# Modulation vectors of a two-layer backbone: other column groups, and another engine for the second layer

## The chip, the cores and the metric

The kernel runs on one core of one Trainium2 chip. The metric is the device time of one execution in microseconds (us); the figure for the kernel before is the median of three runs.

## The reference

Two layers work on 512 latent tokens and 256 context tokens of width 1024, all in float32. Each layer first forms modulation vectors, one set for the latent stream's conditioning vector `c` and one for the context's `c_ctx`:

```python
def ada_mod(cond, w_mod, b_mod):
    return jnp.split(jax.nn.silu(cond) @ w_mod + b_mod, N_MOD, axis=-1)   # w_mod: 1024 x 6144
...
    sh_a, sc_a, gt_a, sh_m, sc_m, gt_m = ada_mod(cond, w_mod, b_mod)
    # pre-norm, input product, three head groups (gated delta rule | global attention | windowed attention)
    x = x + gt_a * (jnp.concatenate([o_a, o_b, o_c], axis=-1) @ w_out)
    x = x + gt_m * sq_relu_mlp(modulate(x, g_mlp, sh_m, sc_m), w_mlp_in, w_mlp_out)
```

The context stream goes the same way in the first layer; in the second it only serves as keys, values and states. The modulation vectors depend on `c`, `c_ctx` and the weights alone.

## The kernel before

Activations are held with features on partitions. Large products are made of float32 parts rounded for the tensor engine: every weight tile of 128x1024 is split into a high and a low part (`weight`, `split`: a copy on ScalarE, a subtraction on VectorE), and `mm3` issues three matmuls for one product. `fm_steps` makes one slice of 128 output features with 24 matmuls of 512 columns (latent) and 24 of 256 (context).

Nothing is issued where it is written. The program is recorded as a list of operations (`Program.add`) with an estimated duration each (`cost`); `layout` then gives every operation a rank, the length of what has to follow it, and plays the five engines forward in time: the operation with the highest rank that is ready and finds memory goes next. The order that results is what each engine gets, as a fixed list. Memory is by kind of tile (`KINDS`: width, and numbers of slots that are always there or in two regions X and Y that change hands between mixers and MLP). `sm`, the staging tile of the modulation weights, has two slots in region X, in the phases of the input products and the mixers only.

One layer is: input products beside the first part of the delta rule; a tail with the rest of the delta rule (`pre`, `scan_step`, `finish`, unit by unit, each state needing the one before) and the attention; the output projection; the MLP, in four rounds of eight slices of hidden features (`w1`) and eight output slices (`w2`). The profile has layer 0's MLP from 810 to 1350 us and layer 1's from 1990 us to the end.

`mod_steps` forms a third (16 columns of 128 features) of a layer's modulation vectors: 16 weight tiles `w_mod` of 128x1024, and for each, two matmuls with the conditioning vectors as the 32-column stationary operand and 512 weight columns streaming. Outputs of 32 rows go to partitions 32j of one PSUM tile, so each matmul uses one of four column groups of the array:

```python
for k in range(KT):
    for hf in range(2):
        st = self.stage(self.a["w_mod"][L.l, r, k, hf], ...)
        for q in range(2):
            j = hf * 2 + q
            nc.tensor.matmul(ps[32 * j:32 * j + 32, :], self.cs[:, k, :], st[:, q * 512:q * 512 + 512], ...)
```

A copy, four transposes and additions of the bias follow, and `aa`, the factors of the norms. The first third of layer 0 is made at the very start. `run` records the others behind the attention: layer 0's second and third third and layer 1's first in layer 0, layer 1's second and third in layer 1. All instructions carry line 674, the helper that issues; tiles tell them apart: `sm` modulation weights, `cs` conditioning vectors, `b` and `h` split activations and hidden features, `w` split weights, `lb` and `kaq` parts of the delta rule's `pre`.

Of the kernel before, what the change touches and what calls it, by code (L numbers as in the profile page):

```python
# [19 lines left out]
P = 128  # L20
# [5 lines left out]
# units of the delta rule: the token tiles that the two directions take at the same time (context first)  # L26
# [7 lines left out]
# Memory by kind of tile: elements per partition, whether rounded for the tensor engine, slots that are always there, and  # L34
# those in two regions that change with the phase (input products, mixers, MLP): X (mixers and before | MLP) and Y
# (input products and MLP | mixers).
# [8 lines left out]
    "pre": (0, False, 0, 1, 0, 0, 0), "inv": (0, False, 0, 1, 0, 0, 0),  # L45
# [3 lines left out]
# how long (ns) before its time, as the length of what follows tells it, an instruction may take memory  # L49
AHEAD = (1e9, 1e9, 1e9, 1e9, 1e5)  # L50
# kinds of which there is little for that
HOARD = ("g", "sm", "t", "u", "a", "r", "kaq", "kv")
# which copies of transposed weights VectorE does, ScalarE the others
# [12 lines left out]
def _constants():  # L66
# [35 lines left out]
    # from here on they are loaded where they are needed  # L102
# [20 lines left out]
# order of the streamed weight tiles of a layer: each [128, 1024] float32  # L123
# [3 lines left out]
def lay_out(inp):  # L127
    """numpy layout only: every array that the chip reads, in its float32 type."""
# [48 lines left out]
class Layer:  # L177
    """What belongs to one layer: small state, arrays in DRAM."""
# [8 lines left out]
class View:  # L187
    """A part of a tile: what the scheduler has to know of it, and how to get it from the real tile."""
# [83 lines left out]
class Tile:  # L272
    """A tile that gets its memory when the program is laid out in time."""
# [18 lines left out]
class Op:  # L292
    __slots__ = "phase", "n", "eng", "name", "args", "kw", "preds", "succs", "tiles", "dur", "moved", "fn", "wait", "ready", "rank", "start", "end", "table", "dense"
# [12 lines left out]
class Program:  # L306
    """Instructions in the order of the arithmetic; laid out in time by the length of what follows each, within the
    memory that there is, and then issued in that order."""

    def __init__(self):  # L310
        self.ops, self.tiles, self.phase, self.latest = [], [], 0, {}
        self.tokens, self.name, self.count = [], "", {}
# [9 lines left out]
    def job(self, name):  # L322
        """A job of this name: each takes its memory after the one of that name before it."""
# [4 lines left out]
    @contextmanager  # L328
    def token(self, kind):
        """At most so many of these at a time as the kind has slots."""  # L330
# [14 lines left out]
    def add(self, eng, name, args, kw):  # L345
# [28 lines left out]
        op.table = None  # L374
# [5 lines left out]
    def cost(op, out, ins):  # L380
        """Estimated time (ns) that it holds its engine; for a transfer, also that of the queues."""
        psum = any(v.tile.kind in ("ps", "pu") for v in ins)
        n = out.cols
        if op.eng == PE:
# [3 lines left out]
            if ins[0].dt == F32R:  # L388
                return k / 2.4 + 2.5, 0
# [19 lines left out]
    def epochs(self):  # L409
        """How often each region has changed at every phase."""  # L410
# [8 lines left out]
    def layout(self):  # L419
# [6 lines left out]
        # a job that needs a token goes on when one of those before it ends  # L426
# [4 lines left out]
        for k, l in chains.items():  # L431
            n = KINDS[k][2] + KINDS[k][3] + max(KINDS[k][5:])
            for t, q in zip(l, l[n:]):
                if t.ops[-1] < q.ops[0]:
                    later.setdefault(t.ops[-1], []).append(q.ops[0])
        for o in reversed(ops):
            own = o.dur + (o.moved + 1550 if o.eng == SP else 0)
            o.rank = own + max((LATE[o.eng][ops[s].eng] + ops[s].rank for s in o.succs + later.get(o.n, [])), default=0.0)
        slotted = [t for t in self.tiles if t.kind in KINDS]
        self.epochs()  # L440
        # slots by kind and place: always there (0), region X (1), region Y (2)
# [8 lines left out]
        # tiles of a time of a region that have to be there, or are  # L450
# [12 lines left out]
        def enter(r, e, now):  # L463
            """Region r changes to its time e, if what it held is done with."""
# [20 lines left out]
        def places(t, now):  # L485
            """(free since, place, slot) that the tile may have."""
# [20 lines left out]
                    # what has been free for the shortest time; a region that changes before what is always there  # L507
# [11 lines left out]
        # what would take memory long before its time  # L519
# [4 lines left out]
        while len(order) < len(ops):  # L524
# [31 lines left out]
            # it goes  # L556
# [1223 lines left out]
```

## Time and profile before

| | |
|---|---|
| median of three runs | 2350.1 us (2349.28 to 2351.54) |
| span of the profiled execution | 2364.2 us |
| time around the span | not shown; the profiled execution's own time is taken as its span |
| TensorE busy | 2185.3 us (92%) |
| VectorE busy | 1419.7 us (60%) |
| ScalarE busy | 907.5 us (38%) |
| GpSimd busy | 592.8 us (25%) |

Busy times are sums over stages with different limits, so the table by stage is the one to read. A matmul of a float32 operand that is not rounded leaves two records, one for each pass. A matmul's recorded duration includes its way through the array, and records overlap.

### The profile page before, as it was taken

What the parts mean: (1) busy time and instruction counts of PE and PEld (TensorE: products, weight loads), DVE (VectorE), ACT (ScalarE), POOL (GpSimd) and SP (SyncE); (2) the same over time, 40 slices, a digit from 0 to 9 for tenths busy, and PEclk for the clock granted to TensorE, in tenths of its full rate; (3) what the DMA queues carried; (4) which work ended last, traced back from release to release, by engine and by line L of the source; (5) the groups of instructions that cost most, each with busy time, mean ns of one, the idle gap of its engine ahead of it and who ended that gap; (6) DMA issues with size and microseconds to landing.
All of it is one profiled execution on the core that took longest, in us unless ns stands there. A gap on an engine that the chain in (4) does not pass through costs nothing. (4 is left out here: it accounts for less than half of the span.)

```text
span 2364.2 us, 46388 instructions
## 1 busy us (share of the span) xinstructions
PE 2185.3 (92%) x18408; PEld 1685.5 (71%) x18408; DVE 1419.7 (60%) x3471; ACT 907.5 (38%) x1748; POOL 592.8 (25%) x1170
## 2 busy tenths in 40 slices
PE   6997999699998899999999899999679988999999
PEld 2785788455646788888888777687536556777777
DVE  4788878867764542332323488999966755334333
ACT  4754423345542431222222375544324444222221
POOL 0274455635320000000000016657653300000000
PEclk7998999789998999999999999999779999999999
DMA  7343324675353121212212325343563332322322
GB/s 274 95 137 89 96 79 127 177 215 179 123 177 101 45 70 58 76 46 71 72 45 76 103 58 166 96 133 101 149 186 120 126 107 72 106 89 94 102 90 80
DMA packets 170744, 260.58 MB, mean 110 GB/s; under 512 B 44448, under 2 KB 107424, under 8 KB 170528
## 3 DMA queue, kind: packets, MB, share of 16 engines
q1 hardware_dynamic: 170528, 257.64, 34.9%
q8 instruction: 144, 2.36, 0.4%
q14 instruction: 72, 0.59, 0.1%
HBM read 220.26 MB, written 37.32 MB: 109 GB/s over the span
## 5 line engine op out<-in xcount | busy, mean ns | idle before, releaser
L674 PE MATMUL ps<-b,w 128*128 128x512 f32 (+1 forms) x3936 | 846.6, 363 | 19.1 <-ACT b L674 10.8
L674 PEld LDWEIGHTS ps<-b,w 128*128 128x128 f32 x3936 | 658.6, 192 | 149.3 <-ACT b L674 13.0
L674 PE MATMUL ps<-h,w 128*128 128x512 f32 (+1 forms) x2304 | 480.7, 357 | 1.9 <-DVE w L674 0.9
L674 PEld LDWEIGHTS ps<-h,w 128*128 128x128 f32 x2304 | 381.5, 188 | 75.0 <-DVE w L674 4.9
L674 ACT ACTIVATE w<-st 128x1024 fp32r<-128x1024 f32 x192 | 198.3, 1055 | 594.4 <-PE ps L674 589.5
L674 DVE TENSOR_TENSOR w<-st,w 128x1024 fp32r<-128x1024 f32 x192 | 236.2, 1258 | 237.3 <-PE ps L674 175.0
L674 POOL TENSOR_TENSOR lb<-l,cst 128x72 fp32r<-128x72 f32 (+7 forms) x768 | 244.9, 355 | 90.7 <-ACT l L674 59.6
L674 ACT ACTIVATE g<-ps 128x512 f32<-128x512 f32 (+3 forms) x286 | 149.8, 540 | 240.1 <-PE ps L674 232.6
L674 DVE SCALAR_TENSOR_TENSOR x<-ps,mod,x 128x512 f32<-128x512 f32 (+1 forms) x120 | 77.0, 658 | 272.2 <-PE ps L674 272.1
L674 PE MATMUL ps<-w,b 128*128 128x256 f32 x1536 | 229.9, 296 | 2.5 <-DVE w L674 2.4
L674 PEld LDWEIGHTS ps<-w,b 128*128 128x128 f32 x1536 | 201.1, 194 | 13.6 <-DVE w L674 4.0
L674 POOL TENSOR_TENSOR g<-g 128x16 f32<-128x16 f32 x12 | 2.3, 226 | 721.9 <-ACT g L674 721.9
L674 DVE TENSOR_TENSOR q<-q,u 128x16 f32<-128x16 f32 (+4 forms) x360 | 133.1, 370 | 22.9 <-ACT u L674 17.7
L674 PE MATMUL ps<-sm,cs 128*32 128x512 f32 x344 | 122.7, 685 | 23.9 <-DMA sm<-w_mod 18.1
L674 DVE TENSOR_TENSOR g<-g 128x512 f32<-128x512 f32 (+3 forms) x112 | 57.8, 541 | 123.1 <-ACT h L674 119.8
L674 DVE SCALAR_TENSOR_TENSOR g<-ps,par,g 128x510 f32<-128x510 f32 (+3 forms) x176 | 106.0, 617 | 7.2 <-ACT g L674 6.4
L674 PE MATMUL ps<-cst,g 128*128 128x128 f32 (+1 forms) x502 | 88.5, 286 | 10.3 <-DVE g L674 6.1
L674 ACT ACTIVATE u<-pu 64x256 f32<-64x256 f32 (+2 forms) x128 | 55.6, 437 | 106.3 <-PE pu L674 93.4
L674 ACT ACTIVATE g<-ps,t 128x256 f32<-128x256 f32 (+2 forms) x144 | 75.3, 532 | 51.0 <-DVE t L674 44.0
L674 POOL TENSOR_TENSOR v<-u,gt 64x256 f32<-64x256 f32 x80 | 52.1, 651 | 142.3 <-DVE t L674 58.2
L674 DVE TENSOR_REDUCE t<-ps 128x2 f32<-128x512 f32 (+3 forms) x104 | 63.2, 622 | 38.6 <-PE ps L674 38.1
L674 PEld LDWEIGHTS ps<-cst,g 128*128 128x128 f32 (+1 forms) x502 | 56.5, 141 | 41.1 <-ACT g L674 15.2
(139 smaller groups left out, 2724.3 us busy)
## 6 DMA issues: line engine op xcount, KB each, us to landing
st<-w SPq DMA_DIRECT2D x128, 512.0 KB, 4.1
sm<-w_mod SPq DMA_DIRECT2D x86, 512.0 KB, 4.3
st<-w_qkv SPq DMA_DIRECT2D x24, 512.0 KB, 4.8
st<-w_tm SPq DMA_DIRECT2D x24, 512.0 KB, 3.8
kv<-kv SPq DMA_DIRECT2D x96, 128.0 KB, 3.5
u<-gd SPq DMA_DIRECT2D x88, 128.0 KB, 3.6
kaq<-kq SPq DMA_DIRECT2D x80, 128.0 KB, 3.2
st<-w_out SPq DMA_DIRECT2D x16, 512.0 KB, 4.5
```

Of the source, the lines that this page charges most:

```text
L674: getattr(engines[o.eng], o.name)(*[real(x) for x in o.args], **{k: real(x) for k, x in o.kw.items()})
```

## The change

Three edits.

1. In `mod_steps`, a weight tile now feeds four matmuls of 256 columns, one in each of the four column groups, instead of two of 512 in two groups; the two halves of a third land side by side in the PSUM tile. This is now used for layer 0 only.
2. Layer 1's modulation vectors are formed in layer 0's MLP by `mod_pieces`: 12 pieces of 512 outputs, each made on VectorE by multiplying eight weight tiles of 128x512 with a per-partition scalar and adding up, for both conditioning vectors (16 operations), then summed over partitions on TensorE with a matrix of ones, copied, transposed and added to the bias. `mlp` takes one piece with every second slice of hidden features until the 12 are used, that is in three of its four rounds. The pieces have a memory kind of their own, `mp` (four slots in the MLP), and the rank of the TensorE work beside which they are recorded (`paced`).
3. The planner's estimate for a rounded matmul of k columns becomes k/2.25 + 4 ns instead of k/2.4 + 2.5.

```diff
+    "mp": (512, False, 0, 0, 4, 0, 0),
...
-                return k / 2.4 + 2.5, 0
+                return k / 2.25 + 4.0, 0
...
+            if o.paced:
+                o.rank = max(o.rank, beside)
+            elif o.eng == PE:
+                beside = o.rank
...
-            for k in range(KT):
-                for hf in range(2):
+            for hf in range(2):
+                for k in range(KT):
...
-                    for q in range(2):
-                        j = hf * 2 + q
-                        nc.tensor.matmul(ps[32 * j:32 * j + 32, :], self.cs[:, k, :], st[:, q * 512:q * 512 + 512],
-                                         start=k == 0, stop=k == KT - 1)
+                    for j in range(4):
+                        nc.tensor.matmul(ps[32 * j:32 * j + 32, 256 * hf:256 * hf + 256], self.cs[:, k, :],
+                                         st[:, j * 256:j * 256 + 256], start=k == 0, stop=k == KT - 1)
...
+    def mod_pieces(self, L):
+        nc = self.nc
+        o, _ = _PAR["b_mod"]
+        for r in range(3):
+            for x in range(4):
+                with self.p.job("mod piece"), self.p.paced():
+                    acc = [self.tile("mp"), self.tile("mp")]
+                    for k in range(KT):
+                        st = self.tile("mp")
+                        self.load(st, self.a["w_mod"][L.l, r, k, x // 2][:, x % 2 * 512:x % 2 * 512 + 512])
+                        for cond in range(2):
+                            c = self.cs[:, k, cond:cond + 1]
+                            if k == 0:
+                                nc.vector.tensor_scalar(acc[cond], st, c, None, op0=ALU.mult)
+                            else:
+                                nc.vector.scalar_tensor_tensor(acc[cond], st, c, acc[cond], op0=ALU.mult, op1=ALU.add)
+                    ps = self.pu()
+                    for cond in range(2):
+                        nc.tensor.matmul(ps[32 * cond:32 * cond + 32, :], self.C("ones")[:, 0:32], acc[cond],
+                                         start=True, stop=True)
+                    sb = self.tile("mp")
+                    self.act(sb[:64], ps[:64], AF.Copy)
+                    tp = self.pu((P, 4, 64))
+                    for b in range(4):
+                        nc.tensor.transpose(tp[:, b], sb[:64, b * P:(b + 1) * P], self.C("ident")[:64, :64])
+                    at = r * 16 + 4 * x
+                    for cond in range(2):
+                        self.tt(L.mod[:, cond, at:at + 4], tp[:, :, 32 * cond], L.pt[:, o + at:o + at + 4], ALU.add)
+                if x == 3:
+                    self.mod_scales(L, r)
+                yield
...
+                if s % 2:
+                    next(beside, None)
...
-            self.mod_steps(L, (1, 2))
             if not L.last:
-                self.mod_begin(layers[L.l + 1])
-                self.mod_steps(layers[L.l + 1], (0,))
+                self.mod_steps(L, (1, 2))
...
-                acc = self.mlp(L, who, xs, y, W)
+                self.mod_begin(layers[L.l + 1])
+                acc = self.mlp(L, who, xs, y, W, beside=self.mod_pieces(layers[L.l + 1]))
```

`mod_scales` holds the lines that formed `aa` in `mod_steps`, unchanged.

## Rows read from the trace of the kernel before

**Rows 1.** page, part 1: engine, busy us (share), number of instructions

```profile
PE 2185.3 (92%) x18408; PEld 1685.5 (71%) x18408; DVE 1419.7 (60%) x3471; ACT 907.5 (38%) x1748; POOL 592.8 (25%) x1170
```

**Rows 2.** busy time by stage: stretch, length, busy us by engine, PEclk, DMA

```profile
430.00:725.00 295.00, 260.69 (x3206) 153.54 (x3202) 215.18 (x785) 126.92 (x358) 123.53 (x273) 0.91 0.56 167
...
810.00:1350.00 540.00, 539.00 (x3060) 468.41 (x3058) 192.94 (x287) 134.45 (x216) 0.00 (x0) 1.00 0.20 66
1350.00:1690.00 340.00, 309.25 (x3691) 249.25 (x3689) 297.38 (x763) 181.74 (x317) 192.01 (x376) 0.96 0.39 114
1690.00:1935.00 245.00, 208.17 (x2564) 126.74 (x2564) 171.13 (x589) 99.14 (x278) 92.52 (x193) 0.88 0.44 132
```

**Rows 3.** the same view, instructions of the tile sm alone

```profile
430.00:725.00 295.00, 68.84 (x192) 8.97 (x192) 0.91 0.56 167
1690.00:1790.00 100.00, 18.95 (x48) 2.12 (x48) 0.74 0.56 158
1690.00:1935.00 245.00, 44.08 (x128) 5.48 (x128) 0.88 0.44 132
```

**Rows 4.** chain of waits from 1690 to 1935 us, shares by line

```profile
by line: PE ps L674 39.8%; PE pu L674 18.3%; DMA sm<-w_mod 10.3%; DVE t L674 6.0%; DVE q L674 3.6%; DMA u<-gd 3.1%; DVE g L674 2.8%; DMA r<-kC 2.8%; DMA a<-kB 2.2%; issue 2.1%; DVE u L674 2.0%; DVE s L674 1.1%; POOL u L674 0.9%; DVE kaq L67
```

**Rows 5.** waits from 430 to 725 us: us, times, longest

```profile
PEld ps L674 <- DMA sm<-w_mod: 9.1, 6, 2.6
...
PE ps L674 <- DMA sm<-w_mod: 5.1, 5, 1.7
```

**Rows 6.** timeline of TensorE in layer 0's mixers: start, length, what

```profile
472.00 1.05 PE L674 MATMUL ps<-sm,cs 128*32 128x512 f32 x2 [1.68 <-DMA sm<-w_mod]
...
474.04 1.04 PE L674 MATMUL ps<-sm,cs 128*32 128x512 f32 x2
...
705.52 1.05 PE L674 MATMUL ps<-sm,cs 128*32 128x512 f32 x4
```

**Rows 7.** timeline of TensorE in the prologue

```profile
39.88 1.05 PE L674 MATMUL ps<-sm,cs 128*32 128x512 f32 x4
```

**Rows 8.** timeline of GpSimd: starts of the bursts on lb

```profile
1456.58 4.20 POOL L674 TENSOR_TENSOR lb<-l,cst 128x72 fp32r<-128x72 f32 x16
...
1489.77 8.24 POOL L674 TENSOR_TENSOR lb<-l,cst 128x72 fp32r<-128x72 f32 x24 [4.02 <-ACT l L674]
...
1798.23 7.56 POOL L674 TENSOR_TENSOR lb<-l,cst 128x72 fp32r<-128x72 f32 x28 [2.02 <-ACT l L674]
...
1856.75 6.51 POOL L674 TENSOR_TENSOR lb<-l,cst 128x72 fp32r<-128x72 f32 x24 [11.48 <-ACT l L674]
```

**Rows 9.** groups of VectorE, 800 to 1345 us: busy, mean ns | idle

```profile
L674 DVE TENSOR_TENSOR w<-st,w 128x1024 fp32r<-128x1024 f32 x63 | 75.1, 1222 | 96.4 <-PE ps L674 68.2 <-issue 20.4 <-ACT w L674 7.7
...
L674 DVE TENSOR_TENSOR h<-g,h 128x512 fp32r<-128x512 f32 x32 | 21.5, 687 | 0.4
...
L674 DVE TENSOR_TENSOR h<-g,h 128x256 fp32r<-128x256 f32 x32 | 13.1, 421 | 0.6
...
L674 DVE SCALAR_TENSOR_TENSOR g<-x,amul,g 128x512 f32<-128x512 f32 x8 | 5.7, 744 | 2.7 <-ACT g L674 2.7
```

**Rows 10.** timeline of TensorE around six transposes of 64 rows

```profile
61.64 0.59 PE L674 MATMUL ps<-cst,g 64*128 64x64 f32 x6
62.15 0.50 PE L674 MATMUL ps<-b,w 128*128 128x512 f32 x1
```

**Rows 11.** waits of TensorE's weight loads, 810 to 1350 us

```profile
PEld ps L674 <- DVE w L674: 2.4, 4, 0.9
```

**Rows 12.** DMA issues, 810 to 1350 us: KB each, median us to landing

```profile
st<-w SPq DMA_DIRECT2D x58, 512.0 KB, 3.9
...
x<-x SPq DMA_DIRECT2D x8, 256.0 KB, 2.4
```

**Rows 13.** busy time in the second MLP

```profile
2050.00:2100.00 50.00, 50.00 (x215) 39.67 (x214) 16.65 (x18) 8.87 (x10) 0.00 (x0) 1.00 0.28 95
```

**Rows 14.** busy time in the first part of layer 1's tail

```profile
1690.00:1790.00 100.00, 75.69 (x883) 44.24 (x884) 71.46 (x207) 28.45 (x70) 51.17 (x98) 0.74 0.56 158
```

More of the change, by code (lines that the diff above doesn't have):

```diff
@@ L292 @@
 class Op:
-    __slots__ = "phase", "n", "eng", "name", "args", "kw", "preds", "succs", "tiles", "dur", "moved", "fn", "wait", "ready", "rank", "start", "end", "table", "dense"
+    __slots__ = "phase", "n", "eng", "name", "args", "kw", "preds", "succs", "tiles", "dur", "moved", "fn", "wait", "ready", "rank", "start", "end", "table", "dense", "paced"
 PE, ACT, DVE, POOL, SP = range(5)
@@ L311, in __init__ @@
         self.ops, self.tiles, self.phase, self.latest = [], [], 0, {}
-        self.tokens, self.name, self.count = [], "", {}
+        self.tokens, self.name, self.count, self.pace = [], "", {}, False
         for e, n in enumerate(("tensor", "scalar", "vector", "gpsimd", "sync")):
@@ L326, in job, with paced @@
         self.name, self.count = old
+    @contextmanager
+    def paced(self):
+        self.pace = True
+        yield
+        self.pace = False
     @contextmanager
@@ L373, in add @@
         op.dense = ins[0].shape[0] / P * (1.0 if outs[0].cols > 64 else 0.6) if eng == PE else 0
-        op.table = None
+        op.table, op.paced = None, self.pace
         if eng == ACT:
@@ L435, in layout @@
                     later.setdefault(t.ops[-1], []).append(q.ops[0])
+        beside = 0.0
         for o in reversed(ops):
@@ L818, in mod_steps @@
         nc = self.nc
-        mod, pm, aa = L.mod, L.pt, L.aa
+        mod, pm = L.mod, L.pt
         o, _ = _PAR["b_mod"]
@@ L835, in mod_steps @@
                 nc.tensor.transpose(tp[:, b * P:(b + 1) * P], sb[:, b * P:(b + 1) * P], self.C("ident"))
-            v = tp.rearrange("p (b j s) -> p b j s", b=4, j=4)
-            bm = pm[:, o + r * 16:o + r * 16 + 16].rearrange("p (j b) -> p b j", j=4)
+            v = tp.rearrange("p (f b j s) -> p f j b s", f=2, b=2, j=4)
+            bm = pm[:, o + r * 16:o + r * 16 + 16].rearrange("p (f j b) -> p f j b", f=2, j=4)
             for cond in range(2):
-                ov = mod[:, cond, r * 16:r * 16 + 16].rearrange("p (j b) -> p b j", j=4)
-                self.tt(ov, v[:, :, :, cond], bm, ALU.add)
@@ L841, in mod_steps @@
-            for w, (sc, gn) in enumerate(((8, "g_attn"), (32, "g_mlp"))):
-                if sc // 16 == r:
-                    go, _ = _PAR[gn]
-                    for cond in range(2):
-                        nc.vector.scalar_tensor_tensor(aa[:, w, cond, :], mod[:, cond, sc:sc + 8], 1.0,
-                                                       pm[:, go:go + 8], op0=ALU.add, op1=ALU.mult)
+                ov = mod[:, cond, r * 16:r * 16 + 16].rearrange("p (f j b) -> p f j b", f=2, j=4)
+                for f in range(2):
+                    self.tt(ov[:, f], v[:, f, :, :, cond], bm[:, f], ALU.add)
@@ new lines, in mod_steps, with mod_scales @@
+            self.mod_scales(L, r)
+    def mod_scales(self, L, r):
+        for w, (sc, gn) in enumerate(((8, "g_attn"), (32, "g_mlp"))):
+            if sc // 16 == r:
+                go, _ = _PAR[gn]
+                for cond in range(2):
+                    self.nc.vector.scalar_tensor_tensor(L.aa[:, w, cond, :], L.mod[:, cond, sc:sc + 8], 1.0,
+                                                        L.pt[:, go:go + 8], op0=ALU.add, op1=ALU.mult)
+    def mod_pieces(self, L):
[15 more added lines that the diff above has]
+                    ps = self.pu()
+                    for cond in range(2):
+                        nc.tensor.matmul(ps[32 * cond:32 * cond + 32, :], self.C("ones")[:, 0:32], acc[cond],
[9 more added lines that the diff above has]
+                if x == 3:
+                    self.mod_scales(L, r)
+                yield
@@ L941, in mlp @@
     @job("mlp")
-    def mlp(self, L, who, xs, y, W, after=None):
+    def mlp(self, L, who, xs, y, W, after=None, beside=iter(())):
         acc = dict.fromkeys(who)
```

## The prediction

> **What bounds the kernel now.** First the page's busy table: TensorE is busy 92% of 2364.2 us, VectorE 60%, the rest less [rows 1]. That average mixes stages, so the next view is the table of busy time by stage [rows 2]. In the first MLP (810 to 1350 us) TensorE is busy 539 of 540 us and VectorE 193: whatever is added to TensorE there lengthens it one for one, while VectorE has room. In the tails of the two mixer stages (430 to 725 us in layer 0, 1690 to 1935 us in layer 1) TensorE is busy 260.7 of 295 and 208.2 of 245 us (88 and 85%), with VectorE at 215.2 and 171.1 (73 and 70%): loaded, but broken up by dependencies. The same table kept to the tile `sm` shows that the modulation matmuls lie in just these two stretches: 68.8 and 44.1 us of TensorE's time [rows 3], 48 tiles in the first and 32 in the second, so 1.43 and 1.38 us a tile.
>
> Are those matmuls on the path there, or do they only fill holes? The chain of waits says that in layer 1 they are on it: of 245 us, 10.3% (25 us) is the wait for a `w_mod` transfer itself, and 58% is TensorE's own work, the modulation matmuls among it [rows 4]. The chain as recovered doesn't reach back to layer 0, so there I read the waits: TensorE's two queues stood 9.1 and 5.1 us for `sm<-w_mod` [rows 5], and the stage is 88% full. TensorE runs its list in order, so each such wait holds up the delta rule's and attention's matmuls listed behind it.
>
> **The change, part by part.** All terms are in the profiled execution's own time. Its span is 2364.2 us; nothing around it is shown, and the runs' median of 2350.1 is 0.994 of it.
>
> *Four column groups in layer 0.* In TensorE's timeline a 512-column product issued alone takes 1.05 and 1.04 us for its two recorded passes (472.00 and 474.04 us), and both products of a weight tile, in two column groups, issued together, also take 1.05 us, all four records (705.52 us) [rows 6]. So groups do run side by side, and half the columns in twice the groups should be half of that, some 0.55 us a tile when the four stand together. The 1.43 us measured per tile contains split pairs and low clock; I halve it to 0.72. Bounds: 0.55 (never split) and 1.43 (always split, nothing gained).
>
> *Prologue.* The first third is bound by its transfers; only what follows the last one counts. The last tile takes 1.05 us from 39.88 us on [rows 7] and becomes about 0.5 shorter; the three before it may gain 0.3 each; two more additions of 16 columns on VectorE cost less than the 0.5 us gained. I take -0.5 us, between nothing and -1.5.
>
> *Tail of layer 0's mixers.* 16 of 48 tiles leave (layer 1's first third) and 32 cost 0.72 instead of 1.43: TensorE sheds 68.8 - 23 = 46 us and would need 215, as much as VectorE's 215 [rows 2, 3]. How much of that shortens the stage? Today's busiest engine reaches 88%; with two engines equally loaded and the same chains I expect less, 80%: 215/0.80 = 269, -26 us. Bounds: 215/0.88 = 244 (-51), and, if chains alone set the length, half of the 14.2 us of waits (-7).
>
> *Tail of layer 1's mixers.* All 32 tiles leave: 208.2 - 44.1 = 164 us on TensorE; VectorE's 171 becomes the larger [rows 2, 3]. 171/0.80 = 214, -31 us. Bounds: 171/0.85 = 201 (-44); at the other end the recurrences of the delta rule alone. Their period shows in GpSimd's bursts on `lb`, one a unit: 33 us apart while input products run beside them (1456.58 to 1489.77), but 58 us for the last interval of this tail (1798.23 to 1856.75) [rows 8]. So the recurrence has been stretched and can shrink; I keep -12 (half of the chain's 25 us of transfer waits) as the small end. No view tells how the planner will reorder what is left.
>
> *The first MLP receives the second layer's 48 tiles* as 12 pieces. On VectorE: 192 operations of 128x512. The nearest row, scalar_tensor_tensor with both tensors in SBUF, takes 744 ns [rows 9]; the 24 plain multiplies are not shown, and I charge them the same (below: nothing, 18 us less). 192 x 0.744 = 143 us; with the present 193 that is 336 of some 565, 60%: hidden behind TensorE as an average. But they come in the halves of the MLP where the hidden slices are formed: this stretch has 64 weight slices, 540/64 = 8.4 us each, so two take TensorE 16.8 us [rows 2] and VectorE 6.9 (twice 1222 + 2 x 687 + 2 x 421 ns [rows 9]), and a piece asks 11.9: 18.8 in 16.8. The excess must wait for the following half, which has more room: 193 - 32 x 3.44 = 83 us used there of 270.
>
> On TensorE, in a stage with no hole: two 32-column products over 512 columns, side by side, 1.05 us as in [rows 6]; four transposes, 0.4 of the 0.59 us that six of that size took [rows 10]; and the break in the stream. *Weighed against a rule:* in that row the 128-row stream goes on at 62.15 us, 0.51 us after the transposes began, so the switch of shape costs under 0.15 us beyond them [rows 10]. The Trainium skill, page "TensorEngine Tiling (Array Packing)", section "Key Properties", says that changing the tiling mode drains the engine and gives no price; two switches a piece would by that rule be on top of the sum; by the row they are under 24 x 0.15 = 3.6 us, and are in it. So 12 x (1.05 + 0.40 + 0.15) = 19 us. Each piece's first product also waits for VectorE's last sum and its transposes for ScalarE's copy; before, TensorE's weight loads waited only 2.4 us for VectorE in this whole stage [rows 11]. I add 0.5 us a piece, 6 us: +25 us together. Bounds: +15 (partly side by side) and +67 (4 us of wait a piece, about the landing time of a 512 KB transfer, 3.9 us [rows 12]).
>
> *Queues.* 48 loads of 512 KB become 96 of 256 KB on SyncE, one list with the MLP's weights. A load waits there for one of two staging slots, and weight loads stand behind it; these run up to two slices (17 us) ahead, against 2.4 us for a 256 KB landing in this stage [rows 12]. Nothing charged; if that cover were gone, the 48-matmul stream would wait, which is the upper bound above. ScalarE's 12 copies are hidden (134 of 540 us busy [rows 2]).
>
> *The planner's new price* of a rounded matmul, 512/2.25 + 4 = 231.6 ns, is what the trace has: 215 of these matmuls in 50 us, 233 ns each [rows 13], against 215.8 in the old formula. It moves instructions everywhere, above all in the stages with TensorE at 91% (50 to 430, 1350 to 1690 us). No row prices that: from nothing to the idle that one such stage has (340 - 309 = 31 us [rows 2]) either way; as each list order has waits of its own, I take 0, within 15 either way.
>
> **Sum:** -0.5 - 26 - 31 + 25 + 0 = -32.5: 2331.7 us in the profile, times 0.994 is 2317.7. I forecast 2318 us, 1.4% less.
>
> **Rivals.**
> *The removed matmuls were filling.* If the tails are bound by recurrence and softmax chains, only waits come back: -0.5 - 8 - 25 + 25 = -8.5, 2342 us. For it: 37 us of TensorE idle in the layer 1 tail in spite of the filler. Against: the chain in [rows 4]. 14%.
> *The clock falls.* Without filler TensorE has longer pauses in the first 100 us of layer 1's tail, where it was granted 0.74 of full clock already, that is 1.2 GHz for half the time [rows 14]. If all of that ran at 1.2 GHz, its other work there (75.7 us busy less 19 of modulation [rows 3, 14]) would lengthen by the half that now runs at 2.4, some 25 us: -32.5 + 25, 2343 us. The Trainium skill's "TensorE: Matmul & The Clock Gate", section "Why this matters for your kernels", says that pauses between bursts return the engine to the lower clock. By that rule this rival would hold; the rows agree in kind, yet attention, which is independent of the recurrence, can move into the pauses. 6%.
> *Slower: VectorE's sums arrive late in the MLP.* TensorE stands 4 us at every piece's product: +67 instead of +25, sum +9.5, 2360 us. It decides from about 3.2 us a piece. For it: 18.8 us asked in 16.8. Against: the sums have 60% of VectorE, and a late piece need only be late in the list. 12%.
> *Better:* both tails at today's 88 and 85%, -51 and -44, with +25: 2280 us; halfway there, 2299 or less, 12%.
> *The spread does nothing* (four groups serialized): layer 0's gain falls by half, 2331 us; inside my range, in the forecast's chance, as is a reordering within 15 us.
>
> **How the numbers follow.** The forecast, 2300 to 2336, has 54%; better 12; filling 14; clock 6; slower 12; the remaining 2 a reordering that costs more. About 0.2% (4.7 us) is what a measurement of this kernel tells from no change. Faster by more than that: 54 + 12 + most of 14 + 6, 0.82; slower 0.13; between, 0.05. The range leaves out the slower rival and the far end of the better one: 2288 to 2350.
>
> **What would show it.** Right: no `sm` tile after 725 us and the out projection of layer 1 some 30 us sooner after its MLP; tiles of eight records in about 0.55 us in layer 0; the first MLP 20 to 30 us longer with TensorE still over 97% busy and VectorE near 60%. Wrong: TensorE waiting for `mp` sums for microseconds at each piece; the tail of layer 1 still near 245 us with new idle time in place of `sm`; granted clock below 0.7 there.

## The result: 1.5% slower, where 1.4% faster was forecast

The changed kernel takes 2387.2 us (median of four runs, 2377.7 to 2390.1) against 2349.7 us for the kernel before in the same comparison: a ratio of 1.0148, interval 1.0117 to 1.0180. The forecast of 2318 and its range up to 2350 were both wrong. The profiled execution after has a span of 2387.9 us against 2364.2, 23.7 longer; the median of before lies 14 us under its own profiled span, which is also longer than every timed execution of that kernel on record (2338.1 to 2359.3 us). So some 14 us of any difference to these stages of before may be that one execution, and the averages over several kernels further down weigh more.

The page of the changed kernel: busy time by engine, then the costliest group that is new, then the DMA issues that are new. L687 is the helper that was L674.

```profile
PE 2159.1 (90%) x18492; PEld 1695.3 (71%) x18492; DVE 1539.6 (64%) x3687; ACT 904.6 (38%) x1749; POOL 604.1 (25%) x1170
...
L687 DVE SCALAR_TENSOR_TENSOR mp<-mp,cs,mp 128x512 f32<-128x512 f32 x168 | 118.4, 746 | 47.6 <-DMA mp<-w_mod 47.5
...
mp<-w_mod SPq DMA_DIRECT2D x96, 256.0 KB, 2.7
```

Against [rows 1], TensorE is 26 us less busy and the kernel is longer all the same; VectorE has 120 us more. The table of busy time by stage, changed kernel, answers to [rows 2]: layer 0's tail, its MLP, layer 1's input products, its tail.

```profile
440.00:708.00 268.00, 224.77 (x2983) 150.73 (x2984) 196.68 (x707) 120.37 (x345) 101.48 (x230) 0.85 0.49 148
...
812.00:1380.00 568.00, 562.49 (x3103) 467.30 (x3102) 289.38 (x458) 138.77 (x220) 0.00 (x0) 1.00 0.31 99
1380.00:1745.00 365.00, 322.90 (x3967) 260.60 (x3967) 320.66 (x816) 181.73 (x323) 220.79 (x416) 0.94 0.38 109
1745.00:1957.00 212.00, 167.36 (x2148) 121.54 (x2148) 144.68 (x530) 93.05 (x264) 72.22 (x154) 0.77 0.25 74
```

The same table for the tile `sm` alone answers to [rows 3]: layer 0's tail, the stretch after it, layer 1's tail.

```profile
440.00:708.00 268.00, 33.30 (x256) 8.31 (x256) 0.85 0.49 148
708.00:1388.00 680.00, 0.00 (x0) 0.00 (x0) 0.98 0.32 103
1745.00:1957.00 212.00, 0.00 (x0) 0.00 (x0) 0.77 0.25 74
```

The reader sees what the forecast asked for: no `sm` after layer 0, tails of 268 and 212 us where there were 295 and 245, an MLP filled to 99% by TensorE with VectorE at 51%. What it did not ask for is in the line of 365 us: the input products of layer 1, whose instructions no edit touches, were 340. To avoid stretches chosen by eye, the table below cuts every run at events of TensorE's timeline: mixers from the first input product of a layer to the first product of its output projection, MLP from there to the first input product of layer 1. Input products end with the last `ps<-w,b`, and the last row ends with the last matmul.

| us | before | after | difference |
|---|---|---|---|
| layer 0 mixers: input products + tail | 375 + 307 | 391 + 271 | +16 - 36 |
| output projection and first MLP | 633 | 680 | +47 |
| layer 1 mixers: input products + tail | 321 + 255 | 353 + 218 | +32 - 37 |
| layer 1 projection and MLP | 424 | 424 | 0 |

The four differences of the mixers sum to -25, the MLP gives +47: +22 of the 23.7. So two things failed: the tails' gain was mostly given back in the stages ahead of them, and the pieces cost nearly twice their forecast. By the medians the kernels are 37.5 us apart; with +47 in the MLP that leaves some 10 us of gain for the mixers, and the 25 hold for these two executions only.

**The pieces on TensorE.** Its timeline in the first MLP of the changed kernel, round one piece (idle time ahead of a group, and who ended it, in brackets):

```profile
845.12 1.04 PE L687 MATMUL pu<-mp,cst 128*32 128x512 f32 x2 [0.86 <-DVE mp L687]
846.10 0.61 PE L687 MATMUL ps<-b,w 128*128 128x512 f32 x2
846.64 1.04 PE L687 MATMUL pu<-mp,cst 128*32 128x512 f32 x2
847.62 1.43 PE L687 MATMUL ps<-b,w 128*128 128x512 f32 x6
848.98 0.46 PE L687 MATMUL pu<-cst,mp 64*128 64x64 f32 x4
```

The two 32-column products do not stand together: ordinary matmuls lie between, and each takes its 0.98 us alone (845.12 to 846.10). So it is in ten of the twelve pieces; two show the four records in one group of 1.05 us. From the starts of all matmuls between 840 and 1360 us I work out the price of a piece, as time from one start to the next: the 40 product records of ten pieces hold 17.6 us and the 40 transposes 4.6, 2.2 us a piece; and the 2750 ordinary matmuls there are 1.6 to 6.8 ns longer each on average than the same kinds in before (233.8, 234.0, 118.6 and 118.8 ns, 840 to 1340 us), 10 us in all, 1.0 a piece. That makes 3.2 us a piece, 39 for twelve.

Those 10 us stand mostly at the changes of shape. Where a 32-column product begins inside the ordinary stream (18 places), the ordinary matmul ahead of it takes a median 91 ns more to the next start than its kind in before, and the first one behind it 104 ns more; round the transposes it is 92 and 103. (The product's own second record takes 523 ns where records inside a group take 453.) These places sum to 6.4 of the 10 us. Waits ahead of the products are 1.9 us, and 1.9 us are spread over ordinary matmuls that border no piece. `after_old_price`, `after_ranks` and `after_one_tile`, described below, have the same medians to 2 ns.

The remaining 8 are mostly waits at the norms ahead of the MLP and behind it, as the waits of TensorE from 708 to 1385 us show (us, times, longest):

```profile
PE ps L687 <- DVE g L687: 6.7, 2, 4.7
PE ps L687 <- DVE b L687: 5.6, 3, 2.4
PE ps L687 <- ACT b L687: 4.2, 2, 3.2
PE pu L687 <- DVE mp L687: 1.5, 2, 0.9
```

The same stage of before, 726 to 1358 us:

```profile
PE ps L674 <- ACT b L674: 5.3, 2, 4.4
PE ps L674 <- DVE g L674: 4.4, 2, 2.6
```

That is 16.5 us for `g` and `b` against 9.7, 7 more: 5 at the norm ahead of the MLP and 2 at the next layer's, behind it. For the late sums of `mp` TensorE waited 1.5 us in all: VectorE wasn't late at the pieces.

**The spread.** TensorE in layer 0's tail, changed kernel:

```profile
463.20 1.08 PE L687 MATMUL ps<-sm,cs 128*32 128x256 f32 x8
...
643.05 0.63 PE L687 MATMUL ps<-sm,cs 128*32 128x256 f32 x6
643.61 0.49 PE L687 MATMUL ps<-r,asel 16*128 16x512 f32 x1
644.03 0.63 PE L687 MATMUL ps<-sm,cs 128*32 128x256 f32 x4
644.59 0.44 PE L687 MATMUL pu<-lb,bdb 128*128 128x384 f32 x1
644.96 0.62 PE L687 MATMUL ps<-sm,cs 128*32 128x256 f32 x2
...
662.37 0.64 PE L687 MATMUL ps<-sm,cs 128*32 128x256 f32 x8
```

Six records (three groups) start and end in the same 0.6 us as two, and a whole tile of eight takes 0.64 at 662 us, where the granted clock is 1.00, so groups do run side by side, near the 0.55 us forecast. But many tiles are split into parts of six, four and two records with other matmuls between, and others run at a lower clock (1.08 us for eight at 463 us, where 0.54 was granted). 32 tiles take 33.3 us of TensorE, 1.04 each, not 0.72.

### The profile page after: what moved, and what is told of

It reads as the page before. It is cut to its first block, busy times and chain, and to the rows that moved or that the text cites. A ratio compares the mean times of both kernels' runs of the same rounds, so it can differ in the third digit from the quotient of the medians.

```text
span 2387.9 us, 46928 instructions
## 1 busy us (share of the span) xinstructions
PE 2159.1 (90%) x18492; PEld 1695.3 (71%) x18492; DVE 1539.6 (64%) x3687; ACT 904.6 (38%) x1749; POOL 604.1 (25%) x1170
## 5 line engine op out<-in xcount | busy, mean ns | idle before, releaser
L687 PE MATMUL ps<-b,w 128*128 128x512 f32 (+1 forms) x3936 | 846.2, 363 | 33.0 <-ACT b L687 12.3
L687 PEld LDWEIGHTS ps<-b,w 128*128 128x128 f32 x3936 | 650.7, 191 | 181.1 <-issue 30.3
L687 PE MATMUL ps<-h,w 128*128 128x512 f32 (+1 forms) x2304 | 480.0, 358 | 1.2 <-ACT w L687 0.9
L687 PEld LDWEIGHTS ps<-h,w 128*128 128x128 f32 x2304 | 379.8, 188 | 78.5 <-ACT w L687 6.3
L687 ACT ACTIVATE w<-st 128x1024 fp32r<-128x1024 f32 x192 | 198.8, 1056 | 611.1 <-PE ps L687 595.9
L687 DVE TENSOR_TENSOR w<-st,w 128x1024 fp32r<-128x1024 f32 x192 | 235.6, 1249 | 207.2 <-PE ps L687 133.8
L687 POOL TENSOR_TENSOR lb<-l,cst 128x72 fp32r<-128x72 f32 (+7 forms) x768 | 249.3, 360 | 68.6 <-ACT l L687 51.9
L687 PE MATMUL ps<-w,b 128*128 128x256 f32 x1536 | 240.4, 300 | 5.6 <-DVE w L687 3.1
L687 DVE SCALAR_TENSOR_TENSOR x<-ps,mod,x 128x512 f32<-128x512 f32 (+1 forms) x120 | 77.3, 658 | 247.5 <-PE ps L687 247.5
L687 PEld LDWEIGHTS ps<-w,b 128*128 128x128 f32 x1536 | 208.9, 199 | 16.4 <-issue 5.1
L687 ACT ACTIVATE g<-ps 128x512 f32<-128x512 f32 (+3 forms) x283 | 147.8, 538 | 166.2 <-PE ps L687 153.1
L687 POOL TENSOR_TENSOR g<-g 128x16 f32<-128x16 f32 x12 | 2.3, 225 | 770.0 <-ACT g L687 770.0
L687 DVE TENSOR_TENSOR q<-q,u 128x16 f32<-128x16 f32 (+4 forms) x360 | 147.5, 410 | 14.1 <-ACT u L687 7.5
L687 DVE SCALAR_TENSOR_TENSOR mp<-mp,cs,mp 128x512 f32<-128x512 f32 x168 | 118.4, 746 | 47.6 <-DMA mp<-w_mod 47.5
L687 DVE SCALAR_TENSOR_TENSOR g<-ps,par,g 128x510 f32<-128x510 f32 (+3 forms) x176 | 105.6, 617 | 4.2 <-ACT g L687 3.6
L687 PE MATMUL ps<-cst,g 128*128 128x128 f32 (+1 forms) x490 | 93.5, 304 | 13.9 <-ACT g L687 11.6
L687 ACT ACTIVATE u<-pu 64x256 f32<-64x256 f32 (+2 forms) x128 | 55.3, 437 | 118.8 <-PE pu L687 100.5
L687 ACT ACTIVATE g<-ps,t 128x256 f32<-128x256 f32 (+2 forms) x144 | 75.5, 531 | 63.2 <-DVE t L687 52.8
L687 ACT ACTIVATE g<-g 128x512 f32<-128x512 f32 (+2 forms) x123 | 65.7, 550 | 62.3 <-DVE g L687 46.8
L687 POOL TENSOR_TENSOR v<-u,gt 64x256 f32<-64x256 f32 x80 | 50.5, 632 | 149.5 <-DVE u L687 97.2
L687 DVE TENSOR_TENSOR g<-g 128x512 f32<-128x512 f32 (+3 forms) x112 | 58.2, 540 | 44.6 <-ACT h L687 38.2
L687 PEld LDWEIGHTS ps<-cst,g 128*128 128x128 f32 (+1 forms) x490 | 60.2, 151 | 37.2 <-ACT g L687 22.9
```

The lines of the kernel that those rows point to most:

```text
L687: getattr(engines[o.eng], o.name)(*[real(x) for x in o.args], **{k: real(x) for k, x in o.kw.items()})
```

## The experiments

Where expectations name a theory by letter: C, the shorter tails lose filler and so TensorE's clock; K, the planner ranks the late input products and attention against the delta rule by what follows, and the moved work upset that ranking; D, VectorE bounds the mixers. Every ratio is against runs of the kernel before on the same chip, with its 95% interval.

**Which edit costs?** Four kernels take the change apart. `price_only` is the kernel before with the new estimate, `after_old_price` the changed kernel with the old one:

```diff
-                return k / 2.4 + 2.5, 0
+                return k / 2.25 + 4.0, 0
```

> The kernel before with only the planner's price of a rounded matmul changed to k/2.25 + 4 ns; every instruction stays, the order changes. Theory P (the new price is what stretched the two stages of input products, whose last product came 17 us later in layer 0 and 32 us later, counted from the layer's first, in layer 1): 20 to 45 us slower, 2370 to 2395. Theory R (the delta rule's chain of units sets the length of the mixers, and the stretched input products are only work that moved): within 10 us of 2350.

> The changed kernel with the old price k/2.4 + 2.5. Theory P: 20 to 45 us faster than the changed kernel, 2342 to 2367. Theory R: as the changed kernel, 2380 to 2395, since pieces and column groups cost and gain the same.

`price_only`: 2365.3 us, 1.0077 (1.0051 to 1.0103). `after_old_price`: 2394.9, 1.0209 (1.0177 to 1.0241). The truer price makes the kernel before 17 us slower, in neither theory's range, and the changed one some 8 us faster, which is R's side. `price_only` has every instruction of before, and still its layer 1 has input products of 343 us and a tail of 234, where before has 321 and 255; the sums are 577 and 576:

```profile
1364.00:1707.00 343.00, 309.77 (x3735) 251.88 (x3736) 302.43 (x776) 174.44 (x311) 196.75 (x380) 0.97 0.39 113
1707.00:1941.00 234.00, 198.74 (x2514) 121.16 (x2512) 160.78 (x571) 99.67 (x276) 87.39 (x190) 0.90 0.45 137
```

So the border between input products and tail moves with the order alone, and a shorter tail by itself says nothing of the total.

`groups_only` is the kernel before with the four column groups for all six thirds, nothing moved:

```diff
-                    for q in range(2):
-                        j = hf * 2 + q
+                    for j in range(4):
...
```

> The kernel before with only the four column groups, for all thirds of both layers, on TensorE where they were. The forecast's reading (TensorE's time in the two tails is on the path): 80 tiles at half of 1.4 us are 55 us less work, so 15 to 35 us faster. Theory R: 0 to 10 us faster, since the unit chain stays.

2337.9 us, 0.9964 (0.9940 to 0.9988): 10 us less in this order, and the only version that does all the work and is faster than both kernels.

`no_mod1` takes layer 1's modulation weights out of the kernel before and puts nothing in their place (the vectors are the bias alone):

```diff
-                self.mod_steps(layers[L.l + 1], (0,))
+                self.mod_bias(layers[L.l + 1])
```

> The kernel before with layer 1's modulation weights left out: its vectors are the bias alone, so 48 loads and 96 products are missing and nothing takes their place. It shows the most that taking them out of the tails can bring. The forecast's reading: 16 tiles leave the first tail and 32 the second, 35 to 45 us faster. Theory R: 5 to 18 us faster.

2352.6 us, 1.0020 (1.0004 to 1.0036). This was the first large surprise: 48 loads and 96 products are gone, and the time isn't shorter at all, which neither theory had. The forecast had 31 us for layer 1's tail and, with its first third, part of the 26 in layer 0. In its profiled execution, at 2338.6 the shortest of its ten runs, the tail of layer 1 did shrink, from 255 us to 213, the input products ahead of it grew from 321 to 336, and layer 0's mixers stayed at 685 for 682. The two spans are 28 us apart where the medians are 3 us apart the other way, so these stages flatter it. The busy table of that tail, `no_mod1`:

```profile
1695.00:1908.00 213.00, 165.43 (x2402) 121.47 (x2400) 161.38 (x570) 100.36 (x281) 93.07 (x190) 0.82 0.27 81
```

**Is it the ranks (K)?** A constant is added to the rank at the step from the mixers to the MLP, so that attention and late input products get back the lead that the moved work gave them:

```diff
+ADD = {1: 33.3e3, 4: 58.6e3}
...
+                    if k == "ps" and t.phase in ADD and q.phase == t.phase + 1:
+                        add[t.ops[-1], q.ops[0]] = ADD[t.phase]
```

> The kernel without layer 1's modulation weights (its vectors are the bias alone), with the planner's ranks put back: the steps that were taken out had stood behind the attention in the chain of PSUM tiles, and without them all attention and late input products weigh 33 us (layer 0) and 51 us (layer 1) less against the delta rule. The constants 33.3 and 58.6 us on the step from mixers to MLP make these ranks those of the kernel before, within 1 us. Theory K (the lost rank is why nothing was gained): 20 to 45 us faster than without the constants, 2305 to 2332. Theory D (VectorE or the unit chain sets the length of the mixers in any order): within 8 us of 2353.

> The changed kernel with the same two constants. Theory K: 20 to 45 us faster than the changed kernel's 2387, 2342 to 2367. Theory D: 2380 to 2395.

> The changed kernel with the old price and the two constants. Theory K: 25 to 50 us faster than 2395, 2345 to 2370. Theory D: 2385 to 2400.

2343.7 (0.9982, 0.9962 to 1.0001), 2389.7 (1.0175, 1.0136 to 1.0215) and 2403.1 us (1.0224, 1.0185 to 1.0263). Nothing comes back in the changed kernel under either price. The constants do move the border (layer 1's input products and tail are 340 + 229 and 326 + 242 us in the two changed kernels, for 353 + 218 and 354 + 221 without them), but the sums stay within 7 us. K falls.

**Are the pieces too dear in their form, or is VectorE late?** `after_narrow` sums each piece by eight products (sixteen records) with one streaming column, straight into the final layout, without copy and transposes. `after_one_tile` keeps one of the eight weight tiles of a piece, so leaves 7/8 of the sums and loads out, and all of TensorE's part in:

```diff
-                        nc.tensor.transpose(tp[:, b], sb[:64, b * P:(b + 1) * P], self.C("ident")[:64, :64])
+                        for cond in range(2):
+                            nc.tensor.matmul(tp[:, b, cond:cond + 1], acc[cond][:, b * P:(b + 1) * P],
+                                             self.C("ones")[:, 0:1], start=True, stop=True)
```

```diff
-                    for k in range(KT):
+                    for k in range(1):
```

> The changed kernel with another sum over partitions in the pieces: eight products of 128 outputs by one column (the sums of VectorE are the stationary operand, a column of ones streams) in place of two 32-column products, a copy and four transposes; no change of the array's shape and no copy in between. Theory S (the MLP's extra length is TensorE time of the pieces, 44 us of stream time around 24 products that stand singly, with the changes of shape): 15 to 25 us faster than 2387. Theory V (the MLP waits for VectorE's late sums): within 6 us of 2387.

> The changed kernel with one of the eight weight tiles summed in each piece: 84 loads and 168 operations on VectorE are left out, TensorE's and ScalarE's part of the pieces stays. Theory S (the first MLP is longer by TensorE's part of the pieces): the first MLP stays at 660 us or more between the first product of the output projection and the first of layer 1, against 633 before, and the time within 15 us of 2387. Theory V (it is longer since VectorE is late): the MLP at 650 or less, 2350 to 2365.

`after_narrow`: 2386.2 us, 1.0151 (1.0112 to 1.0190). Its first MLP is 667 us, 13 less than the changed kernel's, but its layer 1 mixers are 11 longer in another order, so the time falls in V's range without bearing V out. `after_one_tile`: 2369.6, 1.0086 (1.0057 to 1.0115), with a first MLP of 667 too: S by the stage, though the time is 17 us off 2387 where S allowed 15. Its busy table in the MLP:

```profile
821.00:1360.00 539.00, 534.27 (x2941) 445.42 (x2940) 187.19 (x298) 128.38 (x203) 0.00 (x0) 1.00 0.21 68
```

VectorE is back to 187 of 539 us, as in [rows 2], TensorE is still at 99%, and the stage is still 34 us longer than before. Worked out as above (840 to 1345 us, eight pieces), a piece costs 2.3 us in its own matmuls and 0.9 in those beside them: 3.2, as with all the sums in. So what a piece costs inside the MLP is TensorE's own; the sums and loads could account for at most some 13 of the 47 us, none of it at the pieces, and not surely for those: with all the sums in, the changed kernel's other three orders have this stage at 667 to 674 us.

**Clock and filler (C), VectorE (D), or chance?** `no_mod1_fill` is `no_mod1` with the removed products kept, on a resident tile without loads or results. `zero_lo` replaces the low part of every weight by a tile of zeros, which leaves 192 subtractions out of VectorE; it has five slots for weight tiles, which now hold one part each, instead of six. `jitter` is the kernel before with half a nanosecond more in the price of a rounded matmul:

```diff
-                return k / 2.4 + 2.5, 0
+                return k / 2.4 + 3.0, 0
```

```diff
+                        self.nc.tensor.matmul(ps[32 * j:32 * j + 32, :], self.cs[:, k, :], self.cst[:, 0:512], ...)
```

```diff
-        self.split(hi, lo, st)
-        return hi, lo
+        self.act(hi, st, AF.Copy)
+        return hi, self.zero
```

> The kernel without layer 1's modulation weights, but with the 96 products of the three thirds put back where they were, reading a tile that is always there instead of weights (their result is not used): TensorE has the filler, no transfer is waited for. Theory C (without filler TensorE falls to 1.2 GHz in the tails, and that eats the gain: granted clock in layer 1's tail 0.88 before, 0.77 to 0.82 without): faster than both the kernel before and the one without them, 2318 to 2338, clock in the tail back to 0.86 or more. Theory D (VectorE and the unit chain set the length): as without them, 2343 to 2355, whatever the clock. The forecast's reading (their TensorE time is on the path): slower than without them by 20 us or more.

> The kernel before with the low parts of all weights left out: a tile of zeros stands for them, so 192 subtractions of 1.25 us on VectorE are missing (some 30 a layer's mixers can use, 24 weight tiles each), TensorE does the same work. Theory D (VectorE's load sets the length of the mixers): 24 x 1.25 = 30 us of VectorE less in each layer's mixers, 30 to 60 us faster, 2290 to 2318. Theory C and the forecast's reading (TensorE): within 12 us of 2348.

> The kernel before with the planner's price of a rounded matmul 0.5 ns higher (216.3 for 215.8 ns at 512 columns), which says nothing new to it but breaks ties otherwise. Theory O (the order of the kernel before is one of the better ones among many, and any edit that reshuffles loses or wins by chance): 5 to 20 us away from 2348, more likely slower. If order alone does little: within 4 us.

`no_mod1_fill`: 2313.8 us, 0.9855 (0.9830 to 0.9880): with the filler 39 us faster than without, as C wants. But the clock, which is C's cause, didn't rise in the tail that C named: layer 1's, cut as that of `no_mod1` above, has 0.78 against 0.82.

```profile
1664.00:1887.00 223.00, 175.28 (x2397) 128.54 (x2396) 160.52 (x564) 100.60 (x280) 91.90 (x190) 0.78 0.26 76
```

The gain lies in layer 0's mixers (648 us for 685), and in their tail the clock did rise, 0.91 for 0.85. `no_mod1`, then `no_mod1_fill`:

```profile
434.00:729.00 295.00, 243.83 (x3031) 154.57 (x3030) 202.52 (x738) 129.11 (x363) 108.12 (x236) 0.85 0.46 141
430.00:698.00 268.00, 232.81 (x2997) 147.82 (x2996) 199.05 (x728) 126.65 (x363) 109.79 (x235) 0.91 0.50 153
```

Whether filler does that as a rule takes more orders, below.

`zero_lo`: 2350.7, 1.0020 (1.0002 to 1.0038). Its layer 1 mixers, input products and tail, and a stretch of the second MLP:

```profile
1354.00:1685.00 331.00, 305.73 (x3689) 250.60 (x3690) 283.24 (x763) 172.49 (x307) 188.00 (x381) 0.96 0.41 116
1685.00:1923.00 238.00, 198.78 (x2560) 121.28 (x2559) 161.05 (x560) 101.29 (x279) 87.93 (x189) 0.89 0.46 137
2050.00:2100.00 50.00, 50.00 (x217) 40.50 (x216) 9.41 (x13) 13.92 (x16) 0.00 (x0) 1.00 0.33 106
```

The subtractions in the mixers of before, 24 and 23 of them, hold 36 and 29 us of VectorE. Without them the mixers take 686 and 569 us against 682 and 576. The 30 to 60 us that D asked for are not there, in this one order; an order is worth as much (next run), so D is made unlikely, not excluded.

`jitter`: 2384.7, 1.0159 (1.0134 to 1.0184). An estimate moved from 215.8 to 216.3 ns, with the same arithmetic in another order, costs 38 us, as much as the whole change; the expectation was 5 to 20. Its stages by busy time, layer 0's tail to layer 1's:

```profile
440.00:743.00 303.00, 264.35 (x3115) 153.31 (x3115) 205.73 (x754) 122.88 (x351) 118.11 (x259) 0.89 0.52 156
743.00:1375.00 632.00, 618.47 (x3465) 534.35 (x3466) 238.20 (x360) 175.54 (x281) 0.00 (x0) 0.99 0.22 71
1375.00:1694.00 319.00, 299.89 (x3641) 245.85 (x3641) 278.90 (x720) 167.63 (x294) 176.62 (x339) 0.96 0.38 110
1694.00:1956.00 262.00, 206.20 (x2608) 126.07 (x2606) 190.02 (x627) 105.63 (x292) 108.90 (x231) 0.85 0.44 135
```

The MLP is as before; the 21 us between the two profiled spans are in the mixers (698 and 581 us for 682 and 576), whose waits in TensorE are spread over many tiles. The largest (us, times, longest):

```profile
PE pu L674 <- DVE v L674: 35.2, 18, 6.7
PE ps L674 <- DMA sm<-w_mod: 24.6, 13, 4.0
PE pu L674 <- DVE u L674: 18.4, 16, 3.5
```

In before the first was 27.4 us and the last 7.8.

**Three orders of each kernel.** After that, one order of a kernel says little about an edit in the mixers. So three prices were run for those in question: as it was, k/2.4 + 3.0 (`_j`) and k/2.25 + 4.0 (`_p`).

> Without layer 1's modulation weights (its vectors are the bias alone), price k/2.4 + 3.0, at which the kernel before takes 2385. Theory C (the filler keeps TensorE's clock up, and removing it gains little for that): 2340 to 2375, slower than the same with filler by 10 us or more. Theory O (the order decides): anywhere from 2320 to 2390, on either side of the same with filler.

> The same at price k/2.25 + 4, at which the kernel before takes 2365. Theory C: 2335 to 2365, slower than with filler by 10 us or more. Theory O: on either side.

> Without the weights, with the 96 products on a tile that is always there, price k/2.4 + 3.0. Theory C: 2305 to 2345, at least 10 us below the one without filler. Theory O: on either side of it.

> The same at price k/2.25 + 4. Theory C: 2305 to 2345, at least 10 us below the one without filler. Theory O: on either side of it.

> Four column groups for all thirds of both layers, price k/2.4 + 3.0, at which the kernel before takes 2385. If the groups save TensorE time that is on the path: 2355 to 2378. If the order decides: anywhere from 2330 to 2395.

> The same at price k/2.25 + 4, at which the kernel before takes 2365. If the groups save time on the path: 2335 to 2357. If the order decides: anywhere from 2330 to 2395.

| us (ratio) | old price | + 0.5 ns | new price | mean |
|---|---|---|---|---|
| before | 2348 | 2384.7 (1.0159) | 2365.3 (1.0077) | 2366 |
| four groups alone | 2337.9 (0.9964) | 2369.3 (1.0090) | 2361.5 (1.0063) | 2356 |
| without layer 1's | 2352.6 (1.0020) | 2338.0 (0.9951) | 2354.1 (1.0018) | 2348 |
| the same, with filler | 2313.8 (0.9855) | 2349.8 (1.0000) | 2379.4 (1.0126) | 2348 |

The intervals of the six new ratios are 0.9927 to 0.9974, 0.9993 to 1.0042, 0.9983 to 1.0017, 1.0090 to 1.0163, 1.0066 to 1.0114 and 1.0044 to 1.0082, in the order of the texts above. Each row spreads over 16 to 66 us. The filler is worth -39, +12 and +25 us, where C asked for a gain of 10 or more each time. Nor does it raise the clock as a rule: the tail of layer 1 has 0.82, 0.81 and 0.80 without and 0.78, 0.75 and 0.80 with it, that of layer 0 has 0.85, 0.91 and 0.89 without and 0.91, 0.89 and 0.86 with it. C falls; its one success was a lucky order. The order that the kernel before happens to have is the best of its three, 18 us under their mean. Four groups are lower at each price, by 10, 15 and 4 us, but at the last the two intervals overlap, and a mean of 10 us over three orders that spread over 31 to 37 is not shown to be more than chance. Without layer 1's modulation the mean falls by only 18 us, with the same reserve.

The first MLP hardly depends on the draw: 627 to 636 us in the thirteen orders without pieces (`zero_lo` left out), 667 to 680 in the six with them. The four that have whole pieces of the form forecast average 673, 40 us above the three orders of before.

## Why the prediction was wrong

*The step that failed first: "I take 0, within 15 either way" for the planner's price and the reordering.* An order is worth up to 38 us here, and the forecast compared the changed kernel with a favourable one. At the new price the parts stand in a row: price alone +17 us, four groups -4, layer 1 moved +26 (2365.3, 2361.5, 2387.2; by the ratios +18, -3 and +20). At the old price the same move costs 57 us (2337.9 to 2394.9), layer 0's groups being in both. No view of one trace shows such a spread; it takes a second order.

*The tails* were forecast at -26 and -31 us and measured -36 and -37, and that was still the wrong quantity. The step that failed is taking the tail as a stage whose shortening ends in the total: 48 of those us were given back by the input products, +16 and +32, because the planner lets the delta rule, attention and late input products run across that border, which `price_only` moves by 21 us in layer 1 with no instruction changed. The mixers as a whole gained 25 us against 57, and some 10 by the medians. Averaged over the four orders of the changed kernel and three of before, their two stages gain 22 us in the profiled executions; the medians differ by 28 us, which with 40 more in the MLP leaves 12. Taking layer 1's modulation out wholly gains 18 us of time on the mean. The busiest engine's share of a tail did not set the mixers' length.

*The MLP* was forecast at +25 us, bounds 15 to 67, and measured +47 (+40 on the mean of four orders). The mechanism was right, TensorE without a hole; the term was mis-sized. Side by side, as in [rows 6], held for two pieces of twelve, and the matmuls next to a piece lost time too: 39 us in place of 25. The other 8 us, mostly waits at the norms ahead of the MLP and behind it, had no term. VectorE was hidden as forecast, at 51% for the 60 I gave; its sums took 746 ns for 744, the plain multiplies 486 where they were charged the same.

*The column groups.* The Trainium skill, page "TensorEngine Tiling (Array Packing)", section "Key Properties", has a drain at each change of tiling mode. The trace agrees in kind, with a price: 91 ns ahead of a product that stands in the ordinary stream, and 70 and 104 ns behind it. In a piece whose two products stand apart, the ordinary matmuls lose some 0.6 us to switches, and the products 0.14, where the sum had 0.15; the waits ahead of the products are 0.2 us a piece, where it had 0.5. That it is a drain, and nothing else that the change of shape brings, is not shown. The sum names two switches a piece (24 x 0.15 us) and takes in 0.15 for both, where a split piece has six: that was the mis-sized part of the term.

*The rivals.* The one that ended slower, at 2360 us, had the sign and not the cause: `after_one_tile` takes VectorE's sums away and a piece costs the same 3.2 us. "The removed matmuls were filling" comes nearest in the mixers: it has 33 us for the two tails, and the mixers gained 25. "The clock falls" occurred as a fact. The first 100 us of layer 1's tail, against [rows 14]:

```profile
1745.00:1845.00 100.00, 67.69 (x876) 49.05 (x876) 62.95 (x194) 33.13 (x86) 46.01 (x89) 0.64 0.39 112
```

The granted clock is 0.64 there after 0.74, so some 70 us of 100 at 1.2 GHz, with TensorE busy 68 us in place of 76. But the tail is shorter all the same, and over three orders filler restored neither clock nor time as a rule. The chance of 0.82 for a faster kernel rested on a term for the order that the traces of before had not priced.

*What stays open.* Neither TensorE's load, VectorE's, the transfers of `w_mod` nor the ranks was seen to move the mixers' length in a regular way. The unit-by-unit recurrence of the delta rule may set it: in layer 1 the twelve bursts on `lb` start between 58 and 498 us after the layer's first input product before, between 60 and 491 after, though a stage of modulation work has gone. That is argued from two traces, not shown; no run shortened the recurrence alone, and over all twenty traces the last burst starts 470 to 516 us in and layer 1's mixers last 549 to 591, with hardly a link between the two (correlation 0.3). Why the input products grew in just this order stays open too.

## What to carry to other kernels

Where a program plays a list forward by estimated times, every edit also draws a new order: run a null edit, such as half a nanosecond on one price, before believing a difference, and compare edits over several orders. Size what is taken out of a stage by removing it wholly, since work taken from a loaded stage may only let its neighbours spread; what is added to a stage without holes is paid each time, with its switches and pauses. Here the four column groups alone, without the move, are the version to try further; three orders don't prove their gain.

## What was not expected of the hardware

Rounded matmuls in the second MLP stand 217 to 50 us in `zero_lo` and 215 in [rows 13], 230 and 233 ns each, and both MLP stages are some 10 us shorter there. It is not that every matmul became faster: over 280 us near the end the median from start to start of those on `h` is 232 ns in both, while the mean falls from 236 to 232. Those on `b` have a median of 231 to 232 for 232; in the three kernels with filler, whose MLP is that of before, it is 229 to 230. So neither the missing subtractions nor the zeros need be the reason, and what is stays open.

The two records of an unrounded product of 512 columns start 453 ns apart, nearly twice what a rounded matmul takes (233), so it is not shown that each record is a single pass.

A plain multiply of 128x512 took 486 ns where the multiply-add took 746:

```profile
L687 DVE TENSOR_SCALAR mp<-mp,cs x24: 478/486/490, 721.4 to 1153.8; 128x512 f32<-128x512 f32 x24
```
